# Zero matmuls on TensorE while the first blocks load, chunk products grouped by kind, and one load for x 8 and 9

## The chip, the cores and the metric

The kernel runs on one core of one Trainium2 chip. The metric is the device time of one execution in microseconds; the time before is 2038.3 us, the median of three runs from 2037.98 to 2038.63.

A core has five engines that run beside each other, each through its own instructions in order: TensorE (PE in the profile, with its weight loads as PEld) multiplies matrices into the accumulator memory PSUM, VectorE (DVE) and ScalarE (ACT) do elementwise work, GpSimd (POOL) some masks, and SyncE (SP) issues nearly all transfers between the main memory and the on-chip memory SBUF.

## What is computed

One transformer block for 512 positions and a width of 2048, all in float32:

```
h = rmsnorm(x, g_attn)
[qa|ka|va|qb|kb|vb|f] = h @ w_in            # 2048 x (6*1024 + 8)
oa = stick_breaking_attention(qa, ka, va)   # 8 heads of 128
ob = forgetting_attention(qb, kb, vb, log_sigmoid(f + b_f))   # 8 heads of 128
x = x + concat(headnorm(oa), headnorm(ob)) @ w_out
x = x + relu(rmsnorm(x, g_mlp) @ w_up)**2 @ w_down
y = rmsnorm(x, g_final)
```

## The kernel before

**Float32 by three products.** Each float32 operand is cast to a shorter type in which TensorE is fast (the high part, suffix H or h), and what the cast lost is kept as the low part (L or l). A product is then three matmuls: high by high (line 76), weight low by high (line 77) and high by left low (line 78); `mm3` issues them. The cast of a weight block is ScalarE's (`Piece.cast`, line 168), the subtraction that gives its low part is VectorE's (`Piece.low`, line 171). The target of each cast comes from `hi_lo`, which counts its calls in `turn` and takes the next of three rotating pairs (`wh`, `wl`); when a stage has put a spare room in `more_parts`, one call in four gets that room instead:

```
turn[0] += 1
i = turn[0] % (3 + len(more_parts))
if i >= 3:
    return [w[:, :n] for w in more_parts[i - 3]()]
```

The output projection (`out_piece`, lines 1190 to 1194) is the first stage that has a spare room (called `px`, its tile `wx`). Some of its pieces are loaded straight into their pair or room. The count is set anew only ahead of the second half of the last projection (line 1620).

**The first stage.** x is cut into 16 chunks of 128 columns. A chunk k is transposed on TensorE (`turn_x`, line 233, four transpositions into `tr`), scaled and cast on ScalarE (`x_high`, line 236), and its low part made on VectorE (`x_low`, line 239); `x_more`, `x_right` and `x_sum` (lines 242, 245, 248) prepare operands that later products use. The chunk is then multiplied with 264 columns of `w_in` into two PSUM banks (`vy` and `vz`, four blocks of 128 positions): `first_values`, 12 matmuls, block after block. The chunks come in the order 0, 8, 1, 9, 2, 10 and so on.

Weights arrive as pieces: w0 and w8 hold one chunk each (132 KB), the pieces w1 to w7 two chunks each, k and k + 8 (264 KB). A raw piece goes into one of three rotating rooms (`wraw`), so the fourth load has to wait until the first piece has been cast and subtracted, and so on. x arrives by `load_x` (line 221), 256 KB a chunk, into `xa` (chunks 0 to 3 and 8 to 11) and `xb`. SyncE's order of loads is the list `begin`.

**Order.** In this stage the order of TensorE, ScalarE, VectorE and SyncE is written out: each job has a due time in the object `plan`, jobs are sorted by it and issued in that order, and each engine then runs its own in that order. `mm_at` gives the due time of a chunk's products, 6.5 for the first and 1.93 more for each that follows. The due times only order the jobs; nothing waits for a clock. The later stages have TensorE, ScalarE and VectorE in a written order too, except the output projection, where the scheduler of the language places instructions, and SyncE outside the first stage, which it orders as well.

Of the kernel before, what the change touches and what calls it, by code (L numbers as in the profile page):

```python
# [14 lines left out]
P = 128  # L15
NT = 512
TB = NT // P
D = 2048
KC = D // P
# [17 lines left out]
def block_kernel(ctx, tc, x, g_attn, w_in, b_f, g_out_sb, g_out_fox, w_out, g_mlp, w_up, w_down, g_final, y):  # L37
    nc = tc.nc
    pe, act, dve, pool, sp = nc.tensor, nc.scalar, nc.vector, nc.gpsimd, nc.sync

    x = x[0]
# [33 lines left out]
    def mm3(out, sh, sl, mh, ml, first, last):  # L75
        pe.matmul(out, sh, mh, start=first, stop=False, skip_group_check=True)  # L76
        pe.matmul(out, sh, ml, start=False, stop=False, skip_group_check=True)  # L77
        return pe.matmul(out, sl, mh, start=False, stop=last, skip_group_check=True)  # L78
# [23 lines left out]
    g_rows = cp.tile([KC, P], F32, name="g_rows")  # L102
    act.dma_start(g_rows, g_attn[0].rearrange("(h p) -> h p", p=P))
    act.preload_act_table_set("natural_log_exp_and_others")
    g_in = cp.tile([P, KC], F32, name="g_in")
# [28 lines left out]
    hH, hL = ([h4[k // 4][c][:, k % 4, :] for k in range(KC)] for c in range(2))  # L134
# [4 lines left out]
    K8 = KC // 2  # L139

    def v_columns(h):
        return 2 * WSB + h * P if h < NH else o0 + 2 * WSB + (h - NH) * P
# [45 lines left out]
    with ExitStack() as stage:  # L188
# [8 lines left out]
        x12, f5 = (vf.tile([P, K8, 2 * P], F32, tag=f"e{i}", name=name) for i, name in ((1, "x12"), (2, "f5")))  # L197

        def bank(c):
            return vps["xyz".index(c)].tile([P, 2, NT], F32, tag=c, name=f"v{c}")  # L200
# [12 lines left out]
        plan = Plan()  # L213
# [41 lines left out]
        first_ps = [Y[:, 0], Y[:, 1], Z[:, 0], Z[:, 1]]  # L255
        w_rows = w_in.rearrange("(s a p) c -> a p s c", s=2, p=P)
        c0, m = v_columns(order[0]), 2 * P + NH
        w_of = {}

        def first_values(j, piece, i, half):  # L260
            for t in (2 * half, 2 * half + 1):
                ts = slice(t * P, (t + 1) * P)
                mm3(first_ps[t][:, :m], hH[j][:, ts], hL[j][:, ts], piece.hi[:, i, :], piece.lo[:, i, :], j == 0, j == KC - 1)
# [2 lines left out]
        t0, step = 6.5, 1.93  # L266
        mm_at = {j: t0 + step * n for n, j in enumerate(seq)}
        pieces = {}
        for j in (0, K8):
            pieces[j] = Piece(w_rows[0][:, j // K8:j // K8 + 1, c0:c0 + m], 1, m), 0  # L270
        for k in range(1, K8):
            w = Piece(w_rows[k][:, :, c0:c0 + m], 2, m)
            pieces[k], pieces[k + K8] = (w, 0), (w, 1)
        begin = [(load_x, 0, 1), (pieces[0][0].load,), (load_x, 8, 1), (pieces[8][0].load,), (load_x, 1, 1), (load_x, 9, 1),
                 (pieces[1][0].load,), (load_x, 2, 2), (load_x, 10, 2), (pieces[2][0].load,), (pieces[3][0].load,),
                 (load_x, 4, 4), (load_x, 12, 4)]
        for i, (f, *args) in enumerate(begin):
            plan.at(-50 + i, f, *args)
        for k in range(K8):
            t, j = mm_at[k], k + K8  # L280
            for jj, dt in ((k, 0.0), (j, step)):
                for half in range(2):
                    plan.at(t + dt + 0.74 * half, first_values, jj, *pieces[jj], half)
            w = pieces[k][0]
            if k == 0:
                w8 = pieces[8][0]
                jobs = [(-5.0, turn_x, k), (-4.0, x_high, k), (-3.9, w.cast), (-3.5, x_low, k), (-3.4, w.low), (-3.3, x_more, k),
                        (0.1, turn_x, j), (0.2, x_high, j), (0.3, w8.cast), (0.35, x_right, j), (0.4, x_low, j), (0.5, w8.low), (0.6, x_sum, j)]
            else:
                dt = mm_at[k - 1] - t  # L290
                jobs = [(-2.95, turn_x, k), (-2.2, x_high, k), (-1.5, x_low, k), (-0.75, x_more, k),
                        (-1.02, turn_x, j), (-0.3, x_high, j), (0.4, x_right, j), (0.85, x_low, j), (1.6, x_sum, j),
                        (dt + (1.2 if k == 1 else -1.5), w.cast), (dt + (1.3 if k == 1 else -0.05), w.low)]
                if k > 3:
                    jobs.append((-14.0, w.load))
            for dt, f, *args in jobs:
                plan.at(t + dt, f, *args)
        plan.at(-60, columns, g_in, g_rows, KC)
        for t in range(TB):
            plan.at(mm_at[4 + t] + 0.8, square_x, 0, t)  # L300
        quads = {1: {}, 2: {}}
# [184 lines left out]
        for group in (1, 2):  # L486
            t = TV + 7 * TP * (group - 1)
# [49 lines left out]
    with tc.tile_pool(name="att", bufs=1, side="right", reuse_waits="tile") as at, \  # L537
# [14 lines left out]
        plan = Plan()  # L552
# [334 lines left out]
        for n in range(2 * NH + 1):  # L887
            t = TPER * n
            i_s, i_o = n - 1, n - 2
            if n < 2 * NH:  # L890
                pieces = []
# [19 lines left out]
            else:  # L911
                pieces = []
                for a in range(4):
                    c = v_columns(order[2 * NH - 2])
                    k0 = 4 * a
                    w = Piece(w_in[k0 * P:(k0 + 4) * P, c:c + 2 * P].rearrange("(a p) c -> p a c", p=P), 4, 2 * P)
# [3 lines left out]
                for a in range(4):  # L920
                    for tt in range(TB):
                        dt = 1.45 * unit + (0 if unit < 2 else 1.95) + (0 if unit < 13 else 1.1)
# [4 lines left out]
            if 0 <= i_s < 2 * NH:  # L927
                H = heads[i_s]
                ts = t + 6.45 if n < 2 * NH else t + 2.95
# [339 lines left out]
    for db in range(2):  # L1269
# [25 lines left out]
        for i, p in enumerate(G_ORDER):  # L1295
            for m0 in (2,) if db == 0 and p in (1, 2) else (4, 6, 0, 2):
# [5 lines left out]
                if (db or p in (3, 4)) and m0 in (6, 2) and first_loads:  # L1302

                    with tc.issue_after(ins.ins):
                        u, k, a = first_loads.pop(0)
# [232 lines left out]
    def at_step(k):  # L1538
        return (made[steps[k][0]], steps[k][1]) if 0 <= k < len(steps) else (None, None)
# [29 lines left out]
    with tc.manual_schedule(engines={pe.engine, act.engine, dve.engine}):  # L1569
# [5 lines left out]
        for k in range(len(steps)):  # L1575
            n = steps[k][2]
# [6 lines left out]
            w, p = at_step(k - 1)  # L1583
# [23 lines left out]
            w, p = at_step(k)  # L1607
            if w is not None:
                w.multiply(p, rooms.pop(k))
    w, p = at_step(len(steps) - 1)  # L1610
# [34 lines left out]
    pieces = [(p, db) for db in range(2) for p in (2, 3, 7, 4)]  # L1645
# [7 lines left out]
    def down_at(k):  # L1653
        g, db, i, p, u0 = down[k]
        return g, db, i, p, u0, min(2, GROUPS[g][1] - u0)

    with tc.manual_schedule(engines={pe.engine, act.engine, dve.engine}):
        for k in range(-4, len(down)):
            g, db, i, p, u0, m = down_at(max(k, 0))
# [35 lines left out]
            n = GROUPS[g][1]  # L1695
# [7 lines left out]
    g, db, i, p = down[-1][:4]  # L1703
# [150 lines left out]
```

## Time and profile before

| | before |
|---|---|
| runs, median (lowest to highest) | 2038.3 us (2037.98 to 2038.63) |
| profiled execution, its own time | 2037.76 us |
| its span, first to last instruction | 2036.0 us |
| TensorE busy | 2016.1 us (99%) |
| VectorE busy | 1737.6 us (85%) |
| ScalarE busy | 1127.9 us (55%) |
| moved by DMA | 411.88 MB, mean 202 GB/s |

The span is what the trace covers; the execution's own time has 1.76 us more around it. Times inside the trace are counted from the span's start. In the rows, `out<-in` names the tile written and the tiles read, the shape follows, and brackets hold the idle time of that engine just before and what ended it. A busy TensorE is not TensorE at its peak: matmuls overlap, so the spacing of their starts says more than their durations.

### The profile page before, as it was taken

Reading aid. Unit: us, or ns where it says so; the run is one execution under the profiler, and the core shown is the slowest. Engines: PE = TensorE matmul, PEld = TensorE weight load, DVE = VectorE, ACT = ScalarE, POOL = GpSimd, SP = SyncE. Lnnn points to the kernel's source line nnn. Section 1 sums busy time; section 2 is a strip of 40 time slices with the busy share of each in tenths; the row PEclk is TensorE's granted clock in tenths of the full one; section 3 lists DMA queues with packets and bytes.
Section 4 is the critical chain, followed back from the end, with each engine's and each line's share of the span. In section 5 each row is a group of like instructions: output and inputs, shape, how many; then the busy total and the mean of one; then the engine's idle time right before and its main releaser. Section 6 shows DMA issues by size and latency. Waiting matters only on the chain.

```text
span 2036.0 us, 27169 instructions
## 1 busy us (share of the span) xinstructions
PE 2016.1 (99%) x10410; PEld 1741.6 (86%) x10410; DVE 1737.6 (85%) x1966; ACT 1127.9 (55%) x1618; POOL 65.9 (3%) x73
## 2 busy tenths in 40 slices
PE   8999999999999999999999999999999999999998
PEld 8998888888888889988888888888888888888887
DVE  6975777888867688899999999998799888888896
ACT  6543454455554566667667677676644344444444
POOL 0000001100000000000000000000000000000004
PEclk9999999999999999999999999999999999999999
DMA  6417566666537982656666666667685674674642
GB/s 208 164 62 249 191 203 189 210 202 198 185 119 268 302 269 95 210 180 185 215 204 190 214 193 213 197 197 257 241 295 201 225 258 170 235 253 176 222 163 83
DMA packets 269634, 411.88 MB, mean 202 GB/s; under 512 B 10248, under 2 KB 165432, under 8 KB 262976
## 3 DMA queue, kind: packets, MB, share of 16 engines
q1 hardware_dynamic: 268752, 408.04, 60.3%
q10 hardware_dynamic: 752, 2.11, 0.3%
q8 instruction: 82, 1.34, 0.3%
q14 instruction: 48, 0.39, 0.1%
HBM read 313.62 MB, written 96.49 MB: 201 GB/s over the span
## 4 chain that ended last, share of the span: by engine, by line
PE 91%; DVE 5%; DMA 1%; ACT 1%; issue 1%; POOL 0%; SPq 0%; ACTq 0%; DVEq 0%; POOLq 0%
PE psa L1091 10%; PE accd L76 8%; PE accd L77 8%; PE accd L78 8%; PE accq L76 5%; PE accq L78 5%; PE accq L77 5%; PE psa L1089 5%; PE psc L1091 5%; PE psc L1089 3%; PE psb L1091 3%; PE m L76 1%; PE m L77 1%; PE m L78 1%; PE psb L1089 1%; PE accoa L77 1%
## 5 line engine op out<-in xcount | busy, mean ns | idle before, releaser
L1666 ACT CAST wh<-wd 128x1024 fp32r<-128x1024 f32 x126 | 124.9, 998 | 166.7 <-PE accd L78 54.9
L1556 DVE TENSOR_TENSOR wl<-wu,wh 128x1024 fp32r<-128x1024 f32 x157 | 191.5, 1220 | 15.0 <-ACT wh L1550 14.9
L76 PE MATMUL accq<-hH,wh 128*128 128x512 f32 x512 | 201.7, 394 | 0.0
L78 PE MATMUL accq<-hH,wl 128*128 128x512 f32 x512 | 199.7, 390 | 0.0
L77 PE MATMUL accq<-hL,wh 128*128 128x512 f32 x512 | 199.6, 390 | 0.0
L1550 ACT CAST wh<-wu 128x1024 fp32r<-128x1024 f32 x157 | 166.4, 1060 | 47.9 <-PE psc L1091 21.0
L1091 PE MATMUL psa<-f,wh 128*128 128x512 f32 x728 | 181.1, 391 | 0.0
L77 PE MATMUL accd<-wl,uf 128*128 128x512 f32 x436 | 169.6, 389 | 0.0
L78 PE MATMUL accd<-wh,uf 128*128 128x512 f32 x436 | 169.6, 389 | 0.0
L76 PE MATMUL accd<-wh,uf 128*128 128x512 f32 x436 | 169.4, 389 | 0.0
L1091 PEld LDWEIGHTS psa<-f,wh 128*128 128x128 f32 x728 | 133.7, 188 | 25.8
L1673 DVE TENSOR_TENSOR wl<-wd,wh 128x1024 fp32r<-128x1024 f32 x126 | 144.1, 1152 | 13.2 <-ACT wh L1666 13.2
L1440 DVE TENSOR_TENSOR m<-m,accd 128x1024 f32<-128x1024 f32 x84 | 102.3, 1218 | 46.6 <-PE accd L78 46.6
L1666 ACT CAST wx<-wd 128x1024 fp32r<-128x1024 f32 (+1 forms) x82 | 80.8, 995 | 109.0 <-PE accd L78 42.9
L168 ACT CAST wh<-wraw 128x1024 fp32r<-128x1024 f32 (+2 forms) x77 | 76.7, 997 | 67.8 <-PE accq L77 59.5
L78 PEld LDWEIGHTS accq<-hH,wl 128*128 128x128 f32 x512 | 96.1, 188 | 20.3
L77 PEld LDWEIGHTS accq<-hL,wh 128*128 128x128 f32 x512 | 96.2, 188 | 18.6
L76 PEld LDWEIGHTS accq<-hH,wh 128*128 128x128 f32 x512 | 96.2, 188 | 18.5
L76 PE MATMUL accd<-wx,uf 128*128 128x512 f32 x284 | 110.5, 389 | 0.0
L77 PE MATMUL accd<-wx,uf 128*128 128x512 f32 x284 | 110.5, 389 | 0.0
L78 PE MATMUL accd<-wx,uf 128*128 128x512 f32 x284 | 110.5, 389 | 0.0
L1089 PEld LDWEIGHTS psa<-f,wl 128*128 128x128 f32 x728 | 97.0, 191 | 5.9 <-ACT l L1122 0.6
(418 smaller groups left out, 5104.7 us busy)
## 6 DMA issues: line engine op xcount, KB each, us to landing
wu<-in_w_up_dram SPq DMA_DIRECT2D x60, 1024.0 KB, 6.5
ufd<-st SPq DMA_DIRECT2D x98, 512.0 KB, 3.7
wd<-in_w_down_dram SPq DMA_DIRECT2D x48, 1024.0 KB, 8.0
uf<-ufd SPq DMA_DIRECT2D x42, 1024.0 KB, 7.7
wraw<-in_w_in_dram SPq DMA_DIRECT2D x68, 512.0 KB, 4.3
wo<-wsums SPq DMA_DIRECT2D x28, 512.0 KB, 4.7
q<-in_w_in_dram SPq DMA_DIRECT2D x32, 384.0 KB, 5.7
wd<-in_w_down_dram SPq DMA_DIRECT2D x16, 768.0 KB, 6.8
```

The lines of the kernel that those rows point to most:

```text
L76: pe.matmul(out, sh, mh, start=first, stop=False, skip_group_check=True)
L77: pe.matmul(out, sh, ml, start=False, stop=False, skip_group_check=True)
L78: return pe.matmul(out, sl, mh, start=False, stop=last, skip_group_check=True)
L168: act.copy(self.hi, self.source())
L1089: ins = pe.matmul(ps[:, 2 * P:], lo[:, a, :], f_parts(p, a)[0], start=False, stop=last, skip_group_check=True)
L1091: ins = pe.matmul(ps, hi[:, a, :], f_both(p, a), start=a == PAIRS[0] and p in (1, 5), stop=last, skip_group_check=True)
L1440: dve.tensor_tensor(M[p][:, :, db, :], M[p][:, :, db, :], ps, op=ALU.add)
L1550: act.copy(rooms[k][0], srcs[k])
L1556: lows[0] = dve.tensor_tensor(lo, srcs.pop(k), hi.bitcast(F32), op=ALU.subtract)
L1666: act.copy(rooms[k + 3][0], srcs[k + 3])
L1673: dve.tensor_tensor(rooms[k + 2][1], srcs.pop(k + 2), rooms[k + 2][0].bitcast(F32), op=ALU.subtract)
```

## The change

- At the start VectorE sets a block of 128x128 to zero (a slice of `f5`, which is written much later), and TensorE multiplies it by itself, 128x64 a matmul, in plain float32, into a bank that nobody reads: 13 times ahead of everything else, 3 times more between the transposition of chunk 0 and its products.
- The products of chunks 0 and 8 are no longer issued block after block but kind after kind: high by high for all four blocks, then weight low, then left low, with the transpositions of chunks 8, 1 and 9 put between the kinds.
- For chunks 0, 8 and 1 the cast and subtraction of the weights come ahead of those of x. `x_right` of chunk 8 comes behind its `x_low`.
- Chunk 9's weights are a piece of their own (w9), loaded right behind w1, with a cast and a subtraction of its own. So there are ten pieces in this stage instead of nine.
- x 8 and 9 come in one load of 512 KB, the third on the queue; x 9 had a load of its own before, behind x 1.

```
+        still = f5[:, K8 - 1, :P]
+        idle_ps = bank("x")
+        def settle():
+            dve.memset(still, 0.0)
+        def keep_busy(n):
+            for _ in range(n):
+                pe.matmul(idle_ps[:, 0, :P // 2], still, still[:, :P // 2], start=True, stop=True)
+        def first_part(j, piece, i, part):
+            for t in range(TB):
+                ts = slice(t * P, (t + 1) * P)
+                a, b = (hH[j], piece.hi) if part == "hh" else (hH[j], piece.lo) if part == "hl" else (hL[j], piece.hi)
+                pe.matmul(first_ps[t][:, :m], a[:, ts], b[:, i, :], start=j == 0 and part == "hh", stop=False, skip_group_check=True)
...
-        for j in (0, K8):
-            pieces[j] = Piece(w_rows[0][:, j // K8:j // K8 + 1, c0:c0 + m], 1, m), 0
-        for k in range(1, K8):
+        for j in (0, K8, 1, K8 + 1):
+            pieces[j] = Piece(w_rows[j % K8][:, j // K8:j // K8 + 1, c0:c0 + m], 1, m), 0
+        for k in range(2, K8):
...
-        begin = [(load_x, 0, 1), (pieces[0][0].load,), (load_x, 8, 1), (pieces[8][0].load,), (load_x, 1, 1), (load_x, 9, 1),
-                 (pieces[1][0].load,), (load_x, 2, 2), (load_x, 10, 2), (pieces[2][0].load,), (pieces[3][0].load,),
+        begin = [(load_x, 0, 1), (pieces[0][0].load,), (load_x, 8, 2), (pieces[8][0].load,), (load_x, 1, 1),
+                 (pieces[1][0].load,), (pieces[9][0].load,), (load_x, 2, 2), (load_x, 10, 2), (pieces[2][0].load,), (pieces[3][0].load,),
                  (load_x, 4, 4), (load_x, 12, 4)]
...
+                if k == 0:
+                    for part, wait in zip(("hh", "hl", "lh"), (0.0, 0.6, 1.1)):
+                        plan.at(t + dt + wait, first_part, jj, *pieces[jj], part)
+                    continue
                 for half in range(2):
                     plan.at(t + dt + 0.74 * half, first_values, jj, *pieces[jj], half)
...
-                jobs = [(-5.0, turn_x, k), (-4.0, x_high, k), (-3.9, w.cast), (-3.5, x_low, k), (-3.4, w.low), (-3.3, x_more, k),
-                        (0.1, turn_x, j), (0.2, x_high, j), (0.3, w8.cast), (0.35, x_right, j), (0.4, x_low, j), (0.5, w8.low), (0.6, x_sum, j)]
+                jobs = [(-64.5, keep_busy, 13), (-5.0, turn_x, k), (-4.9, keep_busy, 3), (-4.1, w.cast), (-4.0, x_high, k),
+                        (-3.9, w.low), (-3.5, x_low, k), (-3.3, x_more, k), (0.1, turn_x, j), (0.2, w8.cast), (0.25, x_high, j),
+                        (0.3, w8.low), (0.4, x_low, j), (0.6, x_sum, j), (0.85, x_right, j)]
+            elif k == 1:
+                w9 = pieces[9][0]
+                jobs = [(-1.9, turn_x, k), (-1.85, w.cast), (-1.8, x_high, k), (-1.6, w.low), (-1.5, x_low, k), (-0.75, x_more, k),
+                        (-0.8, turn_x, j), (-0.4, w9.cast), (-0.3, x_high, j), (0.3, w9.low), (0.4, x_right, j), (0.85, x_low, j), (1.6, x_sum, j)]
             else:
                 dt = mm_at[k - 1] - t
                 jobs = [(-2.95, turn_x, k), (-2.2, x_high, k), (-1.5, x_low, k), (-0.75, x_more, k),
                         (-1.02, turn_x, j), (-0.3, x_high, j), (0.4, x_right, j), (0.85, x_low, j), (1.6, x_sum, j),
-                        (dt + (1.2 if k == 1 else -1.5), w.cast), (dt + (1.3 if k == 1 else -0.05), w.low)]
+                        (dt - 1.5, w.cast), (dt - 0.05, w.low)]
...
-        plan.at(-60, columns, g_in, g_rows, KC)
+        plan.at(-60, settle)
+        plan.at(-55, columns, g_in, g_rows, KC)
```

## The prediction

> **What bounds the kernel now.** I read the head of the page first, then TensorE's timeline of the first 24 us, ScalarE's and VectorE's beside it, SyncE's queue with its landings, the DMA rate in stretches, and last the one long DMA wait that the waits of TensorE show later.
>
> ```profile
> span 2036.0 us, 27169 instructions
> ...
> PE 2016.1 (99%) x10410; PEld 1741.6 (86%) x10410; DVE 1737.6 (85%) x1966; ACT 1127.9 (55%) x1618; POOL 65.9 (3%) x73
> ```
>
> TensorE is free for 2036.0 - 2016.1 = 19.9 us of the whole span. All that follows the first stage hangs on it in an order written by hand, so what the first stage gains or loses is carried to the end one to one. 0.2% of 2038.3 us is 4.1 us, about what a measurement of this kernel can tell from no change; an edit of the first 20 us has to win nearly everything there to pass that.
>
> TensorE's timeline, one row for an instruction or a run of them (start, duration, in brackets its idle time and who ended it):
>
> ```profile
> 3.66 1.11 PE L233 MATMUL tr<-ident,xa 128*128 128x128 f32 x4
> ...
> 7.29 0.42 PE L76 MATMUL vy<-wh,hH 128*128 128x264 f32 x1
> 7.51 0.42 PE L77 MATMUL vy<-wl,hH 128*128 128x264 f32 x1
> ...
> 14.93 0.60 PE L233 MATMUL tr<-ident,xa 128*128 128x128 f32 x4
> 15.29 0.37 PE L76 MATMUL vy<-wh,hH 128*128 128x264 f32 x1
> 15.49 0.28 PE L77 MATMUL vy<-wl,hH 128*128 128x264 f32 x1
> 15.61 0.34 PE L78 MATMUL vy<-wh,hL 128*128 128x264 f32 x1
> ...
> 16.89 0.60 PE L233 MATMUL tr<-ident,xa 128*128 128x128 f32 x4
> ...
> 23.18 0.28 PE L77 MATMUL vy<-wl,hH 128*128 128x264 f32 x1
> 23.55 0.39 PE L78 MATMUL vy<-wh,hL 128*128 128x264 f32 x1
> ...
> 613.01 0.40 PE L76 MATMUL accoa<-wh,g 128*128 128x512 f32 x1
> 614.62 0.50 PE L77 MATMUL accoa<-wl,g 128*128 128x512 f32 x1 [1.21 <-DMA wl<-wraws]
> ```
>
> The start spacing of equal products is 0.22 us at 7.29 and 0.12 us at 15.49: TensorE begins at half speed (the clock column of the stretches below says 1.00 all along; only the spacing shows it). The row at 15.29 is the first product of chunk 9 (the order is 0, 8, 1, 9, 2, 10, ...); from the transposition at 14.93 to the next at 16.89 a chunk takes 1.96 us, and this pace holds to the end of the stage but for a gap of 0.37 us at 23.18. So the stage's end is set by when chunk 9 starts and by later hitches.
>
> The ScalarE rows show what chunk 9 hangs on; then VectorE's, SyncE's queue, the landing of the load issued at 6.66 (KB, us to landing), and the DMA engines by stretch (clock, busy share, GB/s):
>
> ```profile
> 9.63 0.40 ACT L168 CAST wh<-wraw 128x264 fp32r<-128x264 f32 x1
> 9.93 0.48 ACT L245 ACTIVATE x<-tr,g_in 128x256 f32<-128x256 f32 x1
> ...
> 13.10 0.63 ACT L168 CAST wh<-wraw 128x528 fp32r<-128x528 f32 x1 [1.59 <-DMA wraw<-in_w_in_dram]
> 13.67 0.69 ACT L236 ACTIVATE hH<-tr,g_in 128x512 fp32r<-128x512 f32 x1
> 14.26 0.47 ACT L245 ACTIVATE x<-tr,g_in 128x256 f32<-128x256 f32 x1
> ...
> 21.12 0.63 ACT L168 CAST wh<-wraw 128x528 fp32r<-128x528 f32 x1 [1.03 <-DMA wraw<-in_w_in_dram]
> ```
> ```profile
> 14.76 0.75 DVE L239 SCALAR_TENSOR_TENSOR hL<-tr,g_in,hH 128x512 fp32r<-128x512 f32 x1 [0.28 <-ACT x L245]
> ```
> ```profile
> 4.44 1.96 SPq L221 DMA_DIRECT2D xa<-in_x_dram  x2
> 6.66 5.32 SPq L161 DMA_DIRECT2D wraw<-in_w_in_dram  x2
> ...
> 598.73 0.81 SPq L1194 DMA_DIRECT2D wx<-wraws  x2
> 607.33 0.32 SPq L1194 DMA_DIRECT2D wh<-wraws  x1
> ```
> ```profile
> wraw<-in_w_in_dram SPq DMA_DIRECT2D x1, 264.0 KB, 6.4
> ```
> ```profile
> 2.00:6.00 4.00, 1.00 0.74 201
> 7.00:11.00 4.00, 1.00 1.10 378
> 11.50:14.50 3.00, 1.00 0.74 176
> ```
>
> The weights of chunks 2 and 10 (w2) were issued at 6.66 and landed at 6.66 + 6.4 = 13.06; ScalarE's cast of them, at 13.10, had waited 1.59 us, and it stands ahead of chunk 9's high part (13.67) in ScalarE's order. It stays there after the change: the plan puts w2's cast at 8.86, the new cast of w9 at 9.96, chunk 9's high part at 10.06. **That is my main choice: the change speeds up what comes before chunk 9, and chunk 9 goes on waiting for w2.**
>
> **Chunk 9.** After: from w2's landing W, 0.04 to the cast, 0.57 to the next ScalarE instruction (13.10 to 13.67), 0.30 for the added cast of w9 (9.63 to 9.93), 0.59 for the high part (13.67 to 14.26), 0.50 until VectorE follows (14.26 to 14.76), 0.75 for the low part: W + 2.75. With W as before, 13.06, the first product with a low part starts at 15.81; it started at 15.61. So the start is 0.2 slower at an equal landing, and breaks even at W = 12.86.
>
> What sets W: ahead of and with w2, in both kernels, 8 chunks of x at 256 KB and 792 KB of weights go through one queue, 2840 KB. One load for x 8 and 9 moves the same bytes in half as many rows of double length. At 201 GB/s its 512 KB take 2.6 us, at 378 they take 1.4, so it saves 0 to 1.2 us. Against it: SyncE must hold w9's load until w0's room is free, and behind it stand x 2-3, x 10-11 and w2. Before, that room came free by 6.66 (w2 took it), and the x loads went at 4.44; so they are up to 2.2 us later. w0's cast and subtraction now come before x's, which shortens this, and bytes already issued cover most of it: 0 to 0.5 us. W lies between 11.9 and 13.6. I take 12.7, near the landing that these bytes had, with a third of the saving: **0.2 us gained**, bounds 1.0 gained and 0.7 lost.
>
> **Zero matmuls and order by kind.** 13 + 3 matmuls of 128x64 in plain f32 have no row. The nearest is the transposition at half speed, 1.11 / 4 = 0.28 us; bounds 0.15 (0.60 / 4, full speed) and 0.42 (a product's whole duration). Thirteen from about 1 us take 2.0 to 5.5 us, so the transposition at 3.66 keeps its place or moves up to 2.9 later. The cover: full-speed work from its end, 4.77, to chunk 2's transposition is 0.75 (high part) + 36 products at 0.12 + four transpositions at 0.36 (14.93 to 15.29) = 6.5 us, done by 11.3, while chunk 9's first product waits until W + 0.04 + 0.57 + 0.30 + 0.69 = 14.3. These 3.0 us hide the zero matmuls, and as well a TensorE that stays slow for chunks 0 and 8 (24 x 0.10 = 2.4 us). By the same cover a faster chunk 0 and 8 pay nothing, including the order by kind, which has the same 24 products. If both bad ends met, 2.9 + 2.4 - 3.0 = 2.3 us would show. The VectorE memset falls into its idle start. I count 0.
> The Trainium skill (FP8 and Floating Point Precision, TensorE Precision Notes) says that true fp32 takes four passes; as an estimate from it, 256 columns cost what the 264-column row does, 13 x 0.22 = 2.9 us, also under the cover.
>
> **Loads after w2.** From 11.5 to 14.5 the DMA ran at 176 instead of 378 GB/s, 1.6 us of loading lost: SyncE stood from 6.66 to 11.98 on two issues, the second (w3) waiting for w8's subtraction, with the last 2 MB of x behind it. After, w3 waits for w1's, which comes ahead of chunk 1, so the hole should go and w4's cast (waited 1.03 at 21.12) with it. The rotating pairs shift by one, so that w4's cast must now wait for chunk 10's products; by the plan these end just before it. Then 0.37 - 0.12 = 0.25 us goes at 23.18; bounds 0 and 0.25. **0.2 gained.**
>
> **A side effect at 613 us.** `hi_lo` counts every cast; one more cast shifts its turn for the rest. Calls before w_out: 9 pieces of the first stage, 2 x 7 x 4 of the two groups' products, 16 x 4 of the heads and 4 of the last values, 133, so w_out's first piece was call 134 and the second 135, which as 3 modulo 4 got the spare room wx. That room was loaded at 598.73, the first piece's only from 607.33, and TensorE stood at 613.41. After, the first piece is call 135 and gets wx. The second gets the room of 607.33, needed only after the first piece's products and more. 614.62 - 613.01 less a product's 0.23 is 1.4 us; bounds 0 (another wait right behind, or another order by the scheduler) and 1.4. **1.3 gained.**
>
> **Sum.** 0.2 + 0.2 + 1.3 = 1.7 us: span 2034.3; the execution's own time, 2037.76, becomes 2036.1. The median of the runs lies 0.5 above it, 2036.6.
>
> **Rivals.**
> *Nothing at 613 us* (0.20): the scheduler orders w_out anew, or the next wait takes over. 0.4 us is left, 2037.9. For: a wait removed in a scheduled part often finds a neighbour; against: the turn is plain counting.
> *Loads clearly earlier* (0.14): W = 11.4. 1.5 + 0.2 + 1.3 = 3.0, 2035.3. For: the 201 GB/s of 2 to 6 us leave room; against: x 1 and the weights stay in short rows.
> *The start in full* (0.04): chunk 9 starts at 11.6 instead of 15.29, 3.7 us; with 1.3, 2033.3. It needs W near 9.9, 2840 KB at 368 GB/s from 2 us on, against the 201 of the first four.
> *Slower* (0.12): the held w9 delays w2 past 14.3, where chunk 9 loses more than the 1.5 us gained elsewhere. At W = 14.5 it loses 1.6, and TensorE stands still from 11.3 to 16.1. If that costs it its clock, chunks 9 and 2 run 24 x 0.10 = 2.4 us longer: 1.6 + 2.4 - 1.5 = 2.5 slower, 2040.8. The trace has no stop after the start long enough to show it.
> The Trainium skill (TensorE: Matmul & The Clock Gate, Part 1) has the clock halve after an idle window of about 3.4 us and come back after a busy one; by it the 3.0 us of my forecast are just short of a drop, and this rival's 4.8 us are past it.
>
> **Numbers.** The forecast has 0.50, with its own range 2035.7 to 2039.0 (2.6 gained to 0.7 lost). The range 2034.7 to 2039.9 takes in the two rivals beside it and the lesser part of the slower one. Faster by over 0.2% (under 2034.2) is the full start and an edge of the early loads, 0.06; slower by over 0.2% (over 2042.4) is the end of the slower rival, 0.03; within, 0.91.
>
> **What would show it.** Right: ScalarE's cast of w2 still carries a DMA wait, at 12.2 to 13.2; the two casts and the high part follow it; TensorE idles ahead of chunk 9's first product and chunk 10's transposition is within 1 us of 16.89; no hole in the DMA rate at 11.5 to 14.5; w_out's first products read wx with no DMA wait. Wrong: chunk 9 starting before 13 us (the full start), zero matmuls still running at 6 us, w2 landing after 14, or a new wait between 600 and 640.

## The result and the profile after

The change makes the kernel slower by 3.1 us: a median of 2041.53 us (17 runs, 2040.95 to 2043.34) beside 2038.43 for the kernel before (17 runs, 2037.86 to 2038.94), ratio 1.0017, 95% interval 1.001 to 1.0025. That is 0.15%, inside the 0.2% but clear of noise, since the two sets of runs do not overlap, and above the top of the predicted range. The runs after form two groups, eleven from 2040.95 to 2041.62 (middle 2041.44, 3.0 over the median before) and six from 2042.55 to 2043.34 (middle 2042.9, 4.5 over it); the profiled execution, 2043.34, is of the upper one.

The head of the page after, and TensorE's timeline (start, duration, in brackets the idle time and who ended it):

```profile
span 2041.5 us, 27244 instructions
...
PE 2023.8 (99%) x10442; PEld 1749.8 (86%) x10442; DVE 1738.1 (85%) x1968; ACT 1126.8 (55%) x1619; POOL 64.9 (3%) x73
```
```profile
1.12 5.81 PE L268 MATMUL vx<-f 128*128 128x64 f32 x26 [1.12 <-DVE f L264]
...
7.08 1.11 PE L233 MATMUL tr<-ident,xa 128*128 128x128 f32 x4
7.98 1.38 PE L268 MATMUL vx<-f 128*128 128x64 f32 x6
9.12 0.79 PE L274 MATMUL vy<-wh,hH 128*128 128x264 f32 x2
...
17.01 0.36 PE L76 MATMUL vy<-wh,hH 128*128 128x264 f32 x1
...
26.60 0.39 PE L76 MATMUL vy<-wh,hH 128*128 128x264 f32 x1 [1.32 <-ACT hH L236]
...
27.75 0.39 PE L78 MATMUL vy<-wh,hL 128*128 128x264 f32 x1 [0.64 <-DVE hL L239]
...
30.30 0.42 PE L77 MATMUL vy<-wl,hH 128*128 128x264 f32 x1
30.52 0.42 PE L78 MATMUL vy<-wh,hL 128*128 128x264 f32 x1
...
613.64 0.40 PE L76 MATMUL accoa<-wx,g 128*128 128x512 f32 x1
613.88 0.40 PE L77 MATMUL accoa<-wx,g 128*128 128x512 f32 x1
```

The 13 zero matmuls appear as 26 records, 5.81 us; they hold the transposition of chunk 0 from 3.66 to 7.08. Chunk 9 starts at 17.01 instead of 15.29. New are two stops at 26.6 and 27.8, and behind them products 0.22 us apart: TensorE is at half speed again, from 28.8 to 32.3. At 613 us the first piece reads `wx`, and the wait of 1.21 us is gone.

VectorE, SyncE's queue and ScalarE of the same execution, then the DMA by stretch (the last three columns: clock, busy share, GB/s):

```profile
10.28 0.42 DVE L171 TENSOR_TENSOR wl<-wraw,wh 128x264 fp32r<-128x264 f32 x1
...
13.95 0.43 DVE L171 TENSOR_TENSOR wl<-wraw,wh 128x264 fp32r<-128x264 f32 x1 [0.84 <-ACT wh L168]
```
```profile
10.73 4.05 SPq L161 DMA_DIRECT2D wraw<-in_w_in_dram  x2
14.83 1.01 SPq L221 DMA_DIRECT2D xb<-in_x_dram  x2
```
```profile
14.40 0.94 ACT L168 CAST wh<-wraw 128x528 fp32r<-128x528 f32 x2
...
25.33 0.63 ACT L168 CAST wh<-wraw 128x528 fp32r<-128x528 f32 x1 [3.16 <-DMA wraw<-in_w_in_dram]
```
```profile
7.00:11.00 4.00, 4.00 (x20) 3.96 (x20) 2.27 (x5) 0.99 (x2) 0.00 (x0) 1.00 0.73 220
11.50:14.50 3.00, 3.00 (x26) 3.00 (x26) 1.58 (x3) 1.79 (x5) 0.00 (x0) 1.00 0.68 213
```

The rows are a chain. The subtraction of w8 at 10.28 frees a room, and w2's load goes at 10.73; that of w1 at 13.95 frees the next, w3's load follows, and only behind it, at 14.83 (12.02 before), the last 2 MB of x (`xb`, x 4-7 and 12-15). w4 lies behind these: its cast comes at 25.33, with 3.16 us of waiting for its load, instead of at 21.12. The casts of w2 and w9 at 14.40 wait for no load at all.

### The profile page after: what moved, and what is told of

Read it like the earlier page. It is cut to its first block, busy times and chain, and to the rows that moved or that the text cites. A ratio compares the mean times of both kernels' runs of the same rounds, so it can differ in the third digit from the quotient of the medians.

```text
span 2041.5 us, 27244 instructions
## 1 busy us (share of the span) xinstructions
PE 2023.8 (99%) x10442; PEld 1749.8 (86%) x10442; DVE 1738.1 (85%) x1968; ACT 1126.8 (55%) x1619; POOL 64.9 (3%) x73
## 3 DMA queue, kind: packets, MB, share of 16 engines
q8 instruction: 82, 1.34, 0.3%
## 4 chain that ended last, share of the span: by engine, by line
PE 91%; DVE 5%; DMA 1%; ACT 1%; issue 1%; POOL 0%; ACTq 0%; DVEq 0%; POOLq 0%; SPq 0%
PE psa L1117 10%; PE accd L78 8%; PE accd L76 8%; PE accd L77 8%; PE accq L76 5%; PE accq L78 5%; PE accq L77 5%; PE psa L1115 5%; PE psc L1117 5%; PE psc L1115 3%; PE psb L1117 3%; PE m L76 1%; PE m L78 1%; PE m L77 1%; PE psb L1115 1%
## 5 line engine op out<-in xcount | busy, mean ns | idle before, releaser
L78 PEld LDWEIGHTS accq<-hH,wl 128*128 128x128 f32 x512 | 96.1, 188 | 20.2
```

## The experiments

Each kernel ran in five rounds beside the kernel before on one chip, unless said otherwise; a median is compared with that of the kernel before in the same rounds. At first I held that the zeros cost by what they push back.

**Taking the change apart.** e1_no_zero is the changed kernel without memset and zero matmuls; e2_zero_only has them alone, in the kernel before; e3_turn_only is the kernel before with the count in `hi_lo` begun at one, which is all that the tenth piece does to w_out.

```
e1: -(-64.5, keep_busy, 13),  -(-4.9, keep_busy, 3),  -plan.at(-60, settle)
e2: + still, settle, keep_busy, their three plan entries, columns at -55
e3: -more_parts, turn = [], [0]    +more_parts, turn = [], [1]
```

> The changed kernel without the zeroing and without the 13 + 3 zero matmuls; the rest of the change stays. Theory 1 (the zero matmuls last 5.8 us, hold the transposition of g and with it g_in, which stands ahead of w0's subtraction on VectorE, and so hold w9's load on SyncE and all loads behind it): chunk 0's transposition is back near 3.7 us, w9's load is issued near 5.5 instead of 7.6, w4's weights land near 21 instead of 25.3, TensorE's 1.3 us stop at 26.6 is gone, and the time falls from 2041.5 to 2036.5 to 2037.5. Rival (the extra piece w9 in a queue with three rooms holds the loads by itself): x 2-3 are issued at 7 or later, the stop stays, 2040 or more.

> The kernel before with nothing but the zeroing and the 13 + 3 zero matmuls added. Theory 1: chunk 0's transposition moves from 3.66 to about 7.1, w0's subtraction from 6.2 to about 9.8 and with it w2's load from 6.66 to about 10; x's loads go as before since no piece stands ahead of them; 2 to 4 us slower, 2040.5 to 2042.5. Rival (w9 in the queue is the cause): the loads run on, chunk 0 and 8 catch up, within 1 us of 2038.4.

> The kernel before with the count in hi_lo started at 1 instead of 0, so that only the turn of the pairs and spare rooms is shifted, as one more cast does. If the shift is worth what the prediction said: w_out's first products read wx and have no DMA wait, 1.2 to 1.4 us faster, 2037.0 to 2037.2. Rival (the scheduler orders w_out anew or another wait follows): within 0.4 us of 2038.4.

Beside 2038.29 us before: e1 2037.15 (0.9994, 0.9986 to 1.0003), e2 2042.38 (1.0019, 1.0011 to 1.0028), e3 2037.12 (0.9994, 0.9985 to 1.0003). So the zeros cost 4.1 us alone (e2) and 4.2 in the changed kernel (3.1 slower with them, 1.1 faster without); the shifted turn gains 1.2; the rest of the change is worth nothing on the whole, since e1 and e3 agree within 0.03. The interval of e3 still holds 1, but its 11 runs (2036.92 to 2037.95) lie at the lower edge of the 27 of before (2037.41 to 2039.2): it is the simplest version that beats both kernels in the median, and none that ran beats it clearly. In its trace what it gains lies at w_out: the first stage ends no earlier (the first product behind it, into `vx`, starts at 41.5, and at 41.3 before). The products of the heads at 598 us are still 0.14 us later than before, and the transpositions shortly behind w_out's first products (`pt`) are 1.33 us earlier, first before, then e3:

```profile
618.56 1.26 PE L739 MATMUL pt<-ident,w 128*128 128x128 f32 x10
```
```profile
617.23 1.25 PE L739 MATMUL pt<-ident,w 128*128 128x128 f32 x10
```

**Other data, another type.** e4_ones multiplies ones instead of zeros; e5_r_zero and e6_r_ones use 10 + 3 matmuls of 128x256 in the short type.

```
e4: -dve.memset(still, 0.0)    +dve.memset(still, 1.0)
e5, e6: +dve.tensor_copy(busy, still), busy in hH[15]; pe.matmul(idle_ps[:, 0, :256], busy[:, :P], busy)
        keep_busy 10 in place of 13; zeros in e5, ones in e6
```

> The changed kernel with the block set to one instead of zero: the same matmuls on other data. In the changed kernel 26 records at a spacing of 0.22 us follow each other for 5.8 us and the clock does not rise. If it rises only on data that is not zero: the spacing drops to 0.11 to 0.12 us within these 26, chunk 0's transposition comes 1 to 2 us earlier than 7.08, and the time is 1 to 3 us lower than 2041.5. If plain f32 matmuls do not count whatever their data, or the data does not matter: spacing 0.22 throughout, chunk 0's transposition at 7.1, time unchanged.

> The changed kernel with its busy matmuls in the fast type (fp32r, as the products): 128x256 zeros, 10 ahead and 3 between, at a product's 0.22 us, so 2.2 us from about 1.2 to 3.4 us, no more than the wait for g that stands there anyway. Theory 1 (length is what hurt): chunk 0's transposition is back at 3.7, the loads go as without zero matmuls, 2036 to 2037.5. On the clock: if TensorE's work counts whatever the data, the spacing of chunk 0's or 8's products drops to 0.12 by 8 us (without busy matmuls it dropped at 12.6) and the time is up to 1 us under 2037.15; if zeros do not count, it drops at 12 to 13 as without them, 2037.2.

> The same with ones instead of zeros. If only data that is not zero counts for the clock: the spacing drops by 8 us here and at 12 to 13 with zeros, and this one is up to 1 us faster than with zeros. If data does not matter: both alike, within 0.4 us.

One run of e4 gave 2043.2 us, the same 26 records and the same rows. e5 gave 2039.63 (2038.29 to 2041.44) and e6 2039.87 (2037.94 to 2041.52) beside 2038.23. In e5 the block ends at 4.0, and products reach the 0.12 us spacing at about 10.9; in e6 they have it at 6.1, the first product. That is one execution each, and without any zeros the same spacing comes at about 12.6 in e1 and 10.9 in e13, so only e6 stands out. With TensorE about two microseconds ahead, e6 shows the wait on which my forecast stood:

```profile
12.71 0.95 ACT L168 CAST wh<-wraw 128x528 fp32r<-128x528 f32 x2 [1.30 <-DMA wraw<-in_w_in_dram]
```

w2's cast waits for its load, and chunk 9 starts at 14.30. But `vx` starts at 42.4, later than in e1 (42.0): a faster start pays nothing. Why both are 2.5 us over e1 I could not say then.

**Orders of the loads.** e7_low_first keeps the zeros and puts w0's cast and subtraction ahead of `g_in` on VectorE; e8_order is e1 with w9's load behind x 2-3 and 10-11.

```
e7: w0's cast at -48.6, its subtraction at -48.5, columns at -48.4
e8: (pieces[1][0].load,), (load_x, 2, 2), (load_x, 10, 2), (pieces[9][0].load,), (pieces[2][0].load,)
```

> The changed kernel with all its zero matmuls, but w0's cast and subtraction put ahead of g_in in VectorE's order, so that w9's load no longer waits for the zero matmuls. If the 4.4 us of the zero matmuls come through the loads: w9's load is issued near 5.5 instead of 7.6, w4's weights land near 21.5, TensorE's stop at 26.6 and the drop of its clock behind it are gone, and only the later start of TensorE is left: 2038 to 2039. Rival (they come through TensorE itself, which begins chunk 0 3.4 us late): 2041 or more.

> The changed kernel without zero matmuls, with w9's load put behind x 2-3 and x 10-11 instead of ahead of them. If holding x behind w9 costs: x 2-3 are issued at 4 instead of 6.2, the DMA hole before w3 shrinks, w4's cast waits less at 21.8, and the time is 0.3 to 1 us under the 2037.15 of the run without zero matmuls. If x arrives early enough anyway: within 0.3 us of it.

e7: x 2-3 goes at 5.29 instead of 8.10, but w2 still at 10.72, x 4-7 at 14.81, and 2041.37 us: no gain. e8: 2037.42, no gain over e1.

**How many, and whose room.** e9_dose5 has 5 zeros and not the three, e10_dose13 all 13 and not the three. e11_rooms is the changed kernel with w2 and w3 loaded into rows of `f5` and `x12` that are free till chunk 12; e12_rooms_no_zero the same without zeros.

```
e9:  -keep_busy, 13  +keep_busy, 5;  -(-4.9, keep_busy, 3),      e10: -(-4.9, keep_busy, 3),
e11: Piece.load(place): self.raw = place;  w2 -> f5[:, 4:7], w3 -> x12[:, 4:7]     e12: e11 and e1
```

> The changed kernel with 5 zero matmuls instead of 13, and without the three behind the first transposition. By the theory that only what the zeros push back costs: 5 x 0.446 = 2.2 us from 1.1 end at 3.3, before the wait of TensorE for the first x and for g_rows ends (3.65), so 2037.2 us as without any zeros (2036.9 to 2037.6), chunk 0's transposition at 3.65 to 3.8. By the rival that each zero matmul has a price wherever it stands (4.4 us over 16, 0.275 each): 2038.5.

> The changed kernel with the 13 zero matmuls but without the three behind the first transposition. By the theory the block still ends at 6.9 and chunk 0's transposition at 7.1, but chunk 0's products start at 7.8 to 8.3 instead of 9.12, 1.8 to 2.3 behind the kernel without zeros: 2039.5 to 2040.5. By the price for each matmul: 2040.7. If the three cost nothing: 2041.5.

> The changed kernel, all zeros kept, with w2 and w3 loaded into room of their own (rows of f5 and x12 that are first written by chunk 12's values), so that their loads, and x and w4 behind them on SyncE, no longer wait for the subtractions of w8 and w1. By the theory that the held loads make up what goes beyond chunk 0's 3.1 us: w2 and w3 issued by 9.5, x 4-7 and 12-15 by 10.5 (14.83 now), w4's cast without a wait of 3.2, no second fall of the clock at 29, TensorE's stops at 26.6 and 27.8 gone, and 2038.5 to 2040.6 us, 2040.2 the likeliest. By the rival that the late chunk 0 alone makes it up: the loads earlier and the time still 2041.0 to 2041.8.

> The same rooms of their own for w2 and w3, without the zero matmuls. By the theory that chunk 9 is bound by w2's landing in the changed kernel without zeros and w4's cast by its own: w2 issued by 7 (8.90), w4 by 9 (15.17), w4's wait of 1.1 gone, chunk 9 at 14.5 to 15.3 (15.66), 2036.0 to 2036.9 us. By the rival that the start is bound by the engines' own work: 2037.1, the same within 0.3.

Beside 2038.42: e9 2040.01 (2037.73 to 2041.56), e10 2041.01, e11 2041.18, e12 2039.88 (2036.97 to 2041.61). e9 refutes the theory: five zeros end at 3.5, push chunk 0's transposition from 3.65 to 3.68 only, and still cost. e10: the three between transposition and products cost 0.5 at most, since chunk 0 waits there for ScalarE anyway (its first product at 8.97, with them at 9.12). e11 does what it should to the loads (x 4-7 at 10.19, w4's cast without a wait, no fall of the clock), but w2, now sharing the queue with x, lands later (2.41 us of waiting), and the time stays. The rival's number came out, but not its reason: here chunk 9 does hang on w2, as the prediction had it, and waits for its high part, which stands behind w2's cast:

```profile
18.44 0.39 PE L76 MATMUL vy<-wh,hH 128*128 128x264 f32 x1 [1.24 <-ACT hH L236]
```

In e12 the four lowest runs are at 2036.97 to 2037.9, no better than e1; the six highest, 2039.88 to 2041.61, have no trace and stay unexplained. So loads that come earlier do not help by themselves.

**Is it the zeros, or the chip?** None, 5 and 9 zeros side by side: e13_no_zero_2 (as e1), e14_dose5_2 (as e9), e15_dose9.

> The changed kernel without memset and zero matmuls once more, now beside 5 and 9 zeros on one chip. If the spread of the runs with 5 zeros belongs to the chip, this kernel spreads as far here, from 2036.5 to 2041; if it belongs to the zeros, 2037.2 us within 0.4 and no run above 2038.5.

> The changed kernel with 5 zero matmuls and without the three, again, beside none and 9. By the theory that only what is pushed back costs, its median lies within 0.4 us of the kernel without zeros on the same chip. By the price of 0.275 us for each matmul it lies 1.4 us above. If it lies 2 to 3 us above with a wide spread, the earlier result repeats and the cost is neither of the two, but a state of the loads and stores that the shifted start brings.

> The changed kernel with 9 zero matmuls, without the three: the block ends at 1.1 + 9 x 0.446 = 5.1 us, 1.7 us behind the point at which chunk 0's transposition could start (3.65 becomes 5.3 to 5.4). By the theory the loss is that delay, 1.7 to 2.2 us over the kernel without zeros on the same chip. By the price for each matmul it is 2.5 us.

e13 2037.78 (2036.8 to 2038.41), e14 2040.94 (2039.88 to 2041.65), e15 2040.49 (2039.82 to 2042.07). So it is the zeros, and neither their delay nor a price for each: 5 cost 3.2 us, 9 cost 2.7. Both traces tell where. ScalarE's cast of w4 and, at 790, its first operation on a block of x that SyncE has just stored (`xd`); first e13, then e14:

```profile
21.55 0.63 ACT L168 CAST wh<-wraw 128x528 fp32r<-128x528 f32 x1 [1.41 <-DMA wraw<-in_w_in_dram]
...
790.12 0.63 ACT L1286 ACTIVATE x<-x 128x512 f32<-128x512 f32 x1 [0.35 <-DMA xd<-x]
```
```profile
23.03 0.63 ACT L168 CAST wh<-wraw 128x528 fp32r<-128x528 f32 x1 [2.49 <-DMA wraw<-in_w_in_dram]
...
792.74 0.64 ACT L1287 ACTIVATE x<-x 128x512 f32<-128x512 f32 x1 [2.33 <-DMA xd<-x]
```

Both rows are 1.1 to 2 us more of waiting for a transfer that was issued at the same point of the work. The second weighs more: w4's cast comes 1.5 us later in e14, but by the issue of the store only 0.65 of that is left (788.10 against 787.45), while the row behind it comes 2.6 later and the span is 3.3 longer. The DMA view of 788 to 794 us, 0.15 us a value, for e13 and then e14 (rate; the queue of the data and the queue named instruction, each with packets, MB, share of 16 engines):

```profile
GB/s 0 164 410 437 410 382 410 410 437 410 137 0 0 0 0 0 0 0 0 0 0 0 0 0 0 0 0 0 0 0 0 0 0 0 0 0 0 0 0 0
...
q1 hardware_dynamic: 144, 0.52, 21.3%
q8 instruction: 1, 0.02, 1.4%
```
```profile
GB/s 0 0 0 0 0 0 355 410 519 410 382 410 410 382 109 0 0 27 0 27 0 27 27 27 27 27 27 0 0 0 0 0 0 0 0 0 0 0 0 0
...
q1 hardware_dynamic: 144, 0.52, 21.7%
q8 instruction: 1, 0.02, 1.4%
```

The same 0.52 MB; in e14 the bulk takes about as long, and then a tail of 27 GB/s, a sixteenth of the full rate, runs on for 1.5 us: one of the 16 engines is late with its share. What held it, I read, is the one packet on the instruction queue, 1.4% of 16 engines over 6 us, that is 1.3 us of one engine; the trace does not say which engine a packet is on. By narrow windows it begins in e13 at 789.6, when the store is all but through, in e14 at 789.2, 0.3 us into it. Near 21 us the same: the packet begins at 21.1 in e13 and at 20.3 in e14, and there w4's load ends in the same tail. The page after counts 82 such packets on this queue, q8, with 1.34 MB, 16 KB each. I take them for TensorE's code; no row names the engine, but the count fits. In every trace there are 82, one for about 127 of TensorE's 10410 to 10442 matmul records. The first begins when TensorE has started 106 of them in e13 and 105 in e14, the zeros among them, so ten more in front bring it that much sooner against the work.

**Instructions or run time.** e16_one_wide has one zero matmul of 128x320, e18_two_wide two of 128x416, e17_five_narrow five of 128x4, all without the three.

```
e16: still = f5[:, 4:] as 320 columns; pe.matmul(idle_ps[:, 0, :320], still[:, :P], still); keep_busy 1
e18: the same with 416 columns; keep_busy 2
e17: pe.matmul(idle_ps[:, 0, :4], still, still[:, :4]); keep_busy 5
```

> The changed kernel with one zero matmul of 128x320 in place of the 13 (and without the three): about the run time of five of 128x64 (320 columns x 0.446 / 64 = 2.2 us) in a fifth of the instructions. By the theory of the code load (what costs is how many instructions TensorE gets ahead of its next block of code): near the kernel without zeros, 2037.2 to 2038.2 us, the packet of code near 21 us, w4's cast waiting under 1.6 us and x's store at 790 under 0.5. By the theory that the zeros' run time costs: 2040 to 2041.5, as with five.

> The changed kernel with five zero matmuls of 128x4 in place of the 13 (and without the three): the instructions of five with a small part of their run time (under 1.2 us, done by 2.5). By the theory of the code load: 2040 to 2041.5 us as with five of 128x64, the packet of code at 19.5 to 20.5, w4's cast waiting over 2 us and x's store at 790 over 1.5. By the theory of run time: 2037.2 to 2038.2.

> The changed kernel with two zero matmuls of 128x416 in place of the 13 (and without the three): the 5.8 us of the 13 in a sixth of the instructions, so chunk 0 is pushed back as before (transposition at 7.1 to 7.4) with the code load hardly moved against the work. By the theory that both cost, delay and code load: the delay alone, 3.0 over the kernel without zeros with the room waits of w2 and w3 in it: 2040.2 to 2041.2, w4's cast waiting less than the 3.2 us of the changed kernel. By the theory that delay alone costs: the same as 13 of 128x64, 2041.0 and above.

Beside 2038.62: e16 2037.49, e17 2040.05, e18 2037.46 (2036.28 to 2037.68). TensorE's first rows and w4's cast, e17, then e18:

```profile
1.11 2.30 PE L268 MATMUL vx<-f 128*128 128x4 f32 x10 [1.11 <-DVE f L264]
```
```profile
22.77 0.63 ACT L168 CAST wh<-wraw 128x528 fp32r<-128x528 f32 x1 [2.03 <-DMA wraw<-in_w_in_dram]
```
```profile
1.42 3.14 PE L268 MATMUL vx<-f 128*128 128x416 f32 x4 [1.42 <-DVE f L264]
...
4.70 1.11 PE L233 MATMUL tr<-ident,xa 128*128 128x128 f32 x4
```
```profile
21.49 0.63 ACT L168 CAST wh<-wraw 128x528 fp32r<-128x528 f32 x1 [1.39 <-DMA wraw<-in_w_in_dram]
```

The narrow ones did not do what I meant: 128x4 runs as long as 128x64 (0.23 us a record), so e17 alone parts nothing. Beside it, in the same rounds, e18 does: its zeros run for 3.14 us, longer than e17's 2.30, and even push chunk 0's transposition to 4.70, yet it costs nothing, and its slowest run is faster than e17's fastest; it has 4 records instead of 10. The two wide ones were to last 5.8 us and lasted 3.1, so the full delay without the code shift was not measured. So for zeros of up to 3.1 us it is shown that their run time does not decide. What goes with the cost is their count, though not in proportion: 2 and 4 records cost nothing, 10 cost 2.6 us (e17 beside e18) and 3.2 (e14 beside e13), 18 cost 2.7. That the packet on the late engine is the cause is read from the traces, in which each kernel falls on its side (all columns but the last are of one traced execution):

| kernel | x 4-7 issued | packet begins | w4's cast | issue to cast | first `vx` | median |
|---|---|---|---|---|---|---|
| before | 12.02 | 21.0 | 21.12 | 9.1 | 41.3 | 2038.43 |
| e3, turn only | 12.01 | 21.3 | 21.33 | 9.3 | 41.5 | 2037.12 |
| e1, no zero | 12.49 | 21.7 | 21.83 | 9.3 | 42.0 | 2037.15 |
| e13, no zero | 12.36 | 21.1 | 21.55 | 9.2 | 41.7 | 2037.78 |
| e18, two wide | 12.34 | 21.1 | 21.49 | 9.2 | 41.7 | 2037.46 |
| e6, short type | 11.73 | 19.5 | 22.20 | 10.5 | 42.4 | 2039.87 |
| e14, five | 12.38 | 20.3 | 23.03 | 10.7 | 43.2 | 2040.94 |
| e15, nine | 12.97 | 20.3 | 23.43 | 10.5 | 43.6 | 2040.49 |
| e10, thirteen | 14.69 | 22.5 | 25.18 | 10.5 | 45.3 | 2041.01 |
| after | 14.83 | 20.5 | 25.33 | 10.5 | 47.0 | 2041.53 |
| e2, zeros alone | 15.43 | 21.4 | 25.70 | 10.3 | 45.9 | 2042.38 |

Where the packet begins 8.7 us or more after the issue of x 4-7, w4's cast is 9.1 to 9.3 us behind that issue, in e8 and e16 as well; where it begins 8.0 us or less after it, 10.1 to 10.7, in e4, e5, e7, e9 and e17 as well. w4's own issue does not part them: it is later in e1 (15.17) than in e14 (14.96). And `vx` starts 20.1 to 20.2 us behind w4's cast in every kernel in which the cast waits for its load, 1.5 more where the clock falls again (after, e4, e7). The rows are of before, then after:

```profile
12.02 1.01 SPq L221 DMA_DIRECT2D xb<-in_x_dram  x2
```
```profile
41.28 0.34 PE L76 MATMUL vx<-wh,hH 128*128 128x384 f32 x1
```
```profile
46.99 0.34 PE L76 MATMUL vx<-wh,hH 128*128 128x384 f32 x1
```

**In these kernels w4's landing sets the end of the first stage.** In e11 and e12, where w4's cast (24.02 and 20.67) waits for no load, `vx` is 21.0 behind it; there the stage runs without a stop from chunk 10's transposition, `vx` 24.1 us behind it in both (24.4 before, with the gap at 23.18), so there its end does follow chunk 9.

## Why the prediction was wrong

**The step that failed** is the sentence that the stage's end is set by when chunk 9 starts, and with it the cover of 3.0 us under which the zeros counted 0. In the changed kernel chunk 9 did not even wait for w2, whose cast at 14.40 waits for no load. It does when TensorE is early (e6), but nothing ends there: the stage ends 20.2 us after w4's cast, whose row, with a wait of 1.03 us, I had quoted and priced at 0.25. That cast moved from 21.12 to 25.33, 4.2 us. The two paths are nearly of one length: with w4 early and w2 late (e11) the end goes by chunk 9, as I had it, and is hardly earlier (`vx` at 45.0; 45.3 in e10).

**The zeros' size and path.** I took 0.28 us for each, bounds 0.15 and 0.42; a matmul is two records of 0.223, 0.446 together, and the transposition moved by 3.4 us, past my bound of 2.9, and the zeros still ran at 6 us, which I had named as a sign of being wrong. The sentence from the Trainium skill (FP8 and Floating Point Precision, TensorE Precision Notes) gave 2.9 us for the 13; the trace has 5.81. The delay did not go by TensorE, where I sought the cover, but by the engines behind it: chunk 0 late, the subtractions of w8 and w1 late, the rooms late, and SyncE's queue with x 4-7 and w4. From e13 to after, x 4-7 goes 2.5 us later and w4's cast comes 3.8 later; the other 1.3 I put down to the code packet, as above. About 1 us of delay is indeed free, not 3: in e18 chunk 0's transposition is 1.0 later than in e13 and x 4-7 no later, in e15 it is 1.6 later and x 4-7 0.6.

**The sum, once more.** w4's cast moves by 25.33 - 21.12 = 4.2 us, w_out gives back 1.2: 3.0 slower, as in the eleven lower runs, none of which has a trace. In the profiled one the second fall of the clock adds 1.5 and attention loses another 0.8, most of it in one wait of 0.6 at 176 us; the spans differ by 5.5.

**Loads after w2.** Counted 0.2 gained; the hole moved instead. The rate from 11.5 to 14.5 rose from 176 to 213 GB/s, not to 378, and without zeros w4's cast comes 0.4 to 0.7 later than before. The single load of x 8-9, the order by kind and the piece w9 together brought nothing (e1 against e3).

**613 us.** Right, in place and size: 1.3 counted, 1.2 measured by e3 alone (1.5 at w_out in its trace, part of it lost again later).

**The rivals.** The slower one had the right sign and the wrong place: w2 was late (issued at 10.73; 8.90 in e1, 6.66 before), but it waited for the room of w8 and not behind w9's held load (e7 brought the loads behind w0 forward and w2 still went at 10.72), and w2 was not wanted sooner. The orders meant to bring it earlier gained nothing, but they did not make its cast earlier either (14.38 in e7 beside 14.40; 13.37 in e8 and 13.50 in e12 beside 12.98 in e1). Its other half came, later: TensorE lost its clock, about 1 us behind stops of 1.32 and 0.64 us. The Trainium skill (TensorE: Matmul & The Clock Gate, Part 1) ties the fall to an idle window of about 3.4 us and the rise to as long a busy one; in the profiled run two short stops were enough (the other five of the upper group lie where this fall would put them, but have no trace), and 5.81 us of zeros without a pause did not raise the clock, which came at about 11.6 in this one execution. **That a few more instructions on TensorE would shift what I take for its code loads into other transfers, no part of the prediction had.** By the traces it decides e9, e14 and e17, where w4's cast comes 1.2 to 1.5 us later than in e13, of which 0.5 to 0.7 is left at 788 us, and the wait at 790 is 1.8 to 2.0 longer; and it makes 1.4 of the 4.2 us here (10.5 from issue to cast instead of 9.1).

## What to carry to other kernels

Find which landing the end of a stage follows at a constant distance (here w4's, 20.2 us, wherever its cast waits), and price an edit by what it does to that landing, through rooms and queues, before looking for cover on the engine that the edit sits on. Then ask what binds next: in the kernel before it was chunk 9, 0.25 us behind. Instructions added to fill idle time were not free even where they ended in time (e9); few and large ones were (e18). When a kernel with a harmless edit is slower, look for tails of a sixteenth of the DMA rate and a packet on an instruction queue beside them.

## What the hardware showed that I had not expected

At the start, at half speed, a plain float32 matmul costs 0.22 to 0.23 us a record and two records, for 4 columns as for 64; 320 columns take 1.44 us together, 416 take 1.57. A 16 KB packet on an instruction queue takes 1.0 to 1.4 us in the views above, and a transfer that it meets is waited for 1.1 to 2 us longer (e14 beside e13). Five float32 matmuls ahead move the next such packet by 0.8 us (21.1 in e13 to 20.3 in e14), while two executions without zeros differ by 0.6 (21.7 in e1). Ones in the short type had TensorE at full speed by 6.1 us, zeros not before 10.9, one execution each.
